# Recurrence of a hybrid decoder: both groups of four heads taken through the same stage in every visit

## Chip, core and metric

The kernel runs on one core of one Trainium2 chip. The metric is the device time of one execution in microseconds (us); lower is better. The engines that matter here are TensorE (PE for its matmuls, PEld for its weight loads), VectorE (DVE), ScalarE (ACT) and GpSimd (POOL).

## What is computed

The reference is a decoder trunk of two layers over 256 tokens and 1024 channels, batch 1. Each layer projects the normed input, runs a gated linear recurrence of 8 heads and a sliding-window attention of 16 heads beside each other, merges both under gates, and ends in a feed-forward block. The recurrence is the part that changes (C = 64 rows in a chunk, key and value width 128):

```python
b = jnp.cumsum(fi, axis=2)
o_inter = jnp.einsum('bhtk,bhkv->bhtv', qi * jnp.exp(b), state)
decay = jnp.exp(jnp.where(causal[:, :, None], diff, -jnp.inf))   # diff = b_t - b_s
scores = jnp.einsum('bhtk,bhsk,bhtsk->bhts', qi, ki, decay)
o_intra = jnp.einsum('bhts,bhsv->bhtv', scores, vi)
new_state = jnp.exp(b_last)[..., None] * state + jnp.einsum('bhsk,bhsv->bhkv', ki * jnp.exp(b_last - b), vi)
...
o_hg = rmsnorm(o_hg, hg_norm) * silu(hg);  y_a = o_hg @ w_pa
```

The kernel does not walk over chunks. It builds the whole matrix of decayed scores in levels: blocks of 4 rows, then 16, then pairs of 16, 32 and 64 rows, then the block of the second 128 tokens against the first 128; after each level q and k are multiplied by the decays that the next level needs.

## The kernel before

All large products are three passes of 128x128x512 matmuls over operands split in a high and a low part. The weights stream in from memory; ACT writes the high part of each piece (`wh`), DVE the low part (`wl`), four pieces ahead of the piece that TensorE reads (`used`, `take`, five buffers each). The functions of a layer are generators: `run` takes the main one (the projections) step by step, and a step is six wide matmuls in `form_a`. After every step it counts down the waits of the side generators (`start`), and runs a piece of each whose wait has ended. A number that a side generator yields is thus a distance in steps of the main work. Two side generators matter: `attention` and `recurrence`.

`attention` ends with `turn(3)`, a yield of `YB` = 3, `values(2)` and `values(3)` together, and a yield of 3. It keeps its scores in the tile `sp`. `recurrence` waits until the fourth `attend` was issued, issues `decays` for both groups of four heads (sigmoids, decays f, keys k), yields `YD` = 2, and polls until `attention` has ended. Each group has a generator `chain(g)`. Its pieces are, in order: pk (ACT copies q into the tile `pk`, DVE multiplies three products behind it), then for each stage one piece for TensorE and one for DVE, ACT and POOL. The stages are lb (blocks of 4 rows), lc (16 rows; its operand `p2` is made in the piece after lb, with a copy e1 by ACT and products e2, e3 by DVE), lv of 16, 32 and 64 rows, lx (the 128x128 block), o (output) and ot (transposition, then the split into `oT`).

Before the change group 0 runs one stage ahead of group 1. A visit issues the matmuls of both groups, group 1 first, then group 0's other work, waits a gap, then group 1's, and waits again (`GAPS`). So there are nine visits: lb0; lb1 with lc0; lc1 with lv16 of group 0; and so on to ot1 alone. Digits 0 and 1 behind a stage name its group below.

Within a visit (`pe_order` true) TensorE's instructions are pinned to the order of the program; DVE and ACT instructions are ordered at build time by a list scheduler, by readiness and then by program order, and every engine runs its list in that order on the chip. PSUM banks come by tag: group 0 uses two banks tagged `hg`, group 1 two tagged `at`, which the attention also uses. Group 0's `pk` and `p2` lie in the place of `sp`, group 1's in a place of their own (`pk`). Tiles tagged `hx` (the attention's `akv` and `kT`, later `sx` and `sq`) share four buffers.

Of the kernel before, what the change touches and what calls it, by code (L numbers as in the profile page):

```python
# [7 lines left out]
F32 = mybir.dt.float32  # L8
# [4 lines left out]
ALU = mybir.AluOpType  # L13
AX = mybir.AxisListType

P = 128
D = 1024
S = 256
# [9 lines left out]
EPS = 1e-6  # L28
MIN_F = 1e-30
NRAW, NW = 3, 5  # L30
YB, YD, YQ = 3, 2, 5
YN = (8,), (4, 3, 4), (4, 7), (4, 11)
GAPS = ((8,), (6, 7), (3, 5), (3, 3), (2, 3), (1, 2), (3, 2), (4, 2), (1,))
NEG = -1e30

C_HQ, C_HF, C_HI, C_HG, C_AQ, C_AK, C_GA, C_GB = 0, 1024, 2048, 3072, 4096, 5120, 5632, 6656
# [6 lines left out]
def trunk(ctx, tc, x, norm1, w_in, lb_logits, hg_norm, attn_sinks, w_pa, w_pb, w_o, norm2,  # L43
# [18 lines left out]
    V, A, G, T = (Ordered(e) for e in (nc.vector, nc.scalar, nc.gpsimd, nc.tensor))  # L62
# [9 lines left out]
    sm = ctx.enter_context(tc.tile_pool(name="sm", bufs=2))  # L72
# [3 lines left out]
    def psum(name, tag="mm"):  # L76
        return pp.tile([P, 512], F32, tag=tag, name=name, bufs=4 if tag == "mm" else 2)
# [4 lines left out]
    def ztile(shape, name, tag="z", dt=F32):  # L82
        return sm.tile(shape, dt, tag=tag, name=name, bufs={"z": 4, "hx": 4, "rp": 2}[tag])
# [345 lines left out]
    def layer(l, n1):  # L429
# [53 lines left out]
        def queries(g):  # L483
            for t in range(NT):
                ps = psum(f"qp{l}{t}{g}", "hg" if g else "at")
                for i in range(4):
                    T.transpose(ps[:, i * P:(i + 1) * P], aq[t][:, g * 512 + i * P:g * 512 + (i + 1) * P], ident)
                A.copy(qT[g][:, :, t * P:(t + 1) * P], ps.rearrange("p (i c) -> p i c", i=4))
# [74 lines left out]
        def attention():  # L563
            state["sp"] = sm.tile([P, 2, 4, 384], F32, tag="sp", name=f"sp{l}", bufs=1)
            for t in range(NT):
                rope(aq[t], QH, t)
            yield YQ
            queries(0)
            yield 2
            for n, gaps in enumerate(YN):  # L570
                visit = [values(n - 2, "mm")] if n > 1 else []
                together(*visit, attend(n))
                if n == 3:
                    state["last"] = True
                yield gaps[0]
                if n:
                    turn(n - 1)
                    yield gaps[1]
                if n == 1:
                    queries(1)  # L580
                    yield gaps[2]
            turn(3)
            yield YB
            together(values(2, "at"), values(3, "at"))
            yield 3

        def decays(g):
            f, q, k = fqk[g]
# [10 lines left out]
        def chain(g):  # L599
            f, q, k = fqk[g]  # L600
            tag, st = ("hg", "at")[g], st2[:, g]
            sd = sm.tile([P, 8, 32], F32, tag=f"sd{g}", name=f"sd{l}{g}", bufs=1)

            def mask(m, n, w):
                return cm[:, m:m + w].rearrange("p (o c) -> p o c", o=1).to_broadcast([P, n, w])

            pk = sm.tile([P, 32, 80], F32, tag=("sp", "pk")[g], name=f"pk{l}{g}", bufs=1)
            qb = q.rearrange("p h (b c) -> p (h b) c", c=32)
            f4 = f.rearrange("p h (b n o) -> p (h b) n o", n=8, o=4)
            q4 = q.rearrange("p h (b n o) -> p (h b) n o", n=8, o=4)  # L610
# [7 lines left out]
            for half in range(2):  # L618
                ps = psum(f"lb{l}{g}{half}", tag)[:, :320].rearrange("p (i c) -> p i c", c=80)
                for i in range(4):  # L620
                    h, t = 2 * half + i // 2, i % 2
                    for j in range(4):
                        ts_ = slice(t * P + 32 * j, t * P + 32 * j + 32)
                        T.matmul(ps[32 * j:32 * j + 32, i, :], k[:, h, ts_], pk[:, 8 * h + 4 * t + j, :],
                                 start=True, stop=True)
# [3 lines left out]
            for half in range(2):  # L629
                ps, sh = pss[half], sd[:, 4 * half:4 * half + 4, :]  # L630
# [14 lines left out]
            ku = k.rearrange("p h (n u m) -> p (h n) u m", u=2, m=2)  # L645
            V.tensor_tensor(ku[:, :, 0], ku[:, :, 0], fu[:, :, 1, 0:1].to_broadcast([P, 256, 2]), ALU.mult)
            V.tensor_tensor(fu[:, :, 0, 0], fu[:, :, 0, 0], fu[:, :, 1, 0], ALU.mult)
            p2 = sm.tile([P, 64, 24], F32, tag=("sp", "pk")[g], name=f"p2{l}{g}", bufs=1)
            qg = q.rearrange("p h (n b c) -> p (h n) b c", b=4, c=4)
            kg = k.rearrange("p h (n u b c) -> p (h n u) b c", u=2, b=2, c=4)  # L650
            fg = f.rearrange("p h (n b c) -> p (h n) b c", b=4, c=4)
# [5 lines left out]
            ps = psum(f"lc{l}{g}", tag)[:, :384].rearrange("p (i n c) -> p i n c", n=2, c=24)  # L657
            for i in range(8):
                h, t = i // 2, i % 2
# [18 lines left out]
            V.tensor_tensor(kg[:, :, 0], kg[:, :, 0], fu[:, :, 1, 0:1].to_broadcast([P, 64, 8]), ALU.mult)  # L678
            V.tensor_tensor(fu[:, :, 0, 0], fu[:, :, 0, 0], fu[:, :, 1, 0], ALU.mult)
            yield  # L680
            m = 16
            while m <= 64:
                nb = S // (2 * m)
                qv = q.rearrange("p h (n u m) -> p (h n) u m", u=2, m=m)
                kv_ = k.rearrange("p h (n u m) -> p (h n) u m", u=2, m=m)
                fv = f.rearrange("p h (n u m) -> p (h n) u m", u=2, m=m)
                ps = psum(f"lv{l}{g}{m}", tag)[:, :64 * 8 if m == 64 else 32 * 8].rearrange("p (i c) -> p i c", i=8)
                for i in range(8):
                    h, a = i // 2, i % 2 * P
                    if m == 16:  # L690
                        for j in range(4):
                            ts_ = slice(a + 32 * j, a + 32 * j + 32)
                            T.matmul(ps[32 * j:32 * j + 32, i, :], k[:, h, ts_], q[:, h, ts_], start=True, stop=True)
                    elif m == 32:
                        for j in range(2):
                            b = a + 64 * j
                            T.matmul(ps[64 * j:64 * j + 32, i, :], k[:, h, b:b + 32], q[:, h, b + 32:b + 64],
                                     start=True, stop=True)
                    else:
                        T.matmul(ps[0:64, i, :], k[:, h, a:a + 64], q[:, h, a + 64:a + P], start=True, stop=True)  # L700
                yield
                if m == 32:
                    for j in range(2):
                        A.copy(st[64 * j:64 * j + 32, :, 64 * j + 32:64 * j + 64], ps[64 * j:64 * j + 32])
                    for j in range(4):
                        pr = slice(32 * j, 32 * j + 32)
                        A.copy(st[pr, :, pr], sd[pr])
                elif m == 64:
                    A.copy(st[0:64, :, 64:128], ps[0:64])
                if m < 64:  # L710
                    bc = [P, 4 * nb, m]
                    V.tensor_tensor(qv[:, :, 1], qv[:, :, 1], fv[:, :, 0, 0:1].to_broadcast(bc), ALU.mult)
                    V.tensor_tensor(kv_[:, :, 0], kv_[:, :, 0], fv[:, :, 1, 0:1].to_broadcast(bc), ALU.mult)
                    V.tensor_tensor(fv[:, :, 0, 0], fv[:, :, 0, 0], fv[:, :, 1, 0], ALU.mult)
                else:
                    q4 = q.rearrange("p h (n m) -> p h n m", m=m)
                    k4 = k.rearrange("p h (n m) -> p h n m", m=m)
                    f4 = f.rearrange("p h (n m) -> p h n m", m=m)
                    V.tensor_tensor(q4[:, :, 3], q4[:, :, 3], f4[:, :, 2, 0:1].to_broadcast([P, 4, m]), ALU.mult)
                    V.tensor_tensor(k4[:, :, 0], k4[:, :, 0], f4[:, :, 1, 0:1].to_broadcast([P, 4, m]), ALU.mult)  # L720
                if m == 16:
                    V.copy_predicated(sd, mask(48, 8, 32), ps)
                yield
                m *= 2
            ps = psum(f"lx{l}{g}", tag).rearrange("p (i c) -> p i c", c=P)
            for h in range(4):
                T.matmul(ps[:, h, :], k[:, h, 0:P], q[:, h, P:S], start=True, stop=True)
            yield
            sx = ztile([P, 4, P], f"sx{l}{g}", "hx")
            A.copy(sx, ps)  # L730
            yield
            pss = []
            for t in range(NT):
                ps = psum(f"o{l}{g}{t}", tag).rearrange("p (h c) -> p h c", c=P)
# [9 lines left out]
            for t in range(NT):  # L744
                ps = pss[t]
# [23 lines left out]
        def recurrence():  # L769
            while "last" not in state:  # L770
                yield 1
            for g in range(2):
                decays(g)
            yield YD
            while atd[0] is not None:
                yield 1
            chains = [chain(g) for g in range(2)]
            next(chains[0])
            yield 2
            for n, gaps in enumerate(GAPS):  # L780
                live = [c for g, c in enumerate(chains) if 0 <= n - g < len(GAPS) - 1]
                pe_order[0] = True
                for c in live[::-1]:
                    next(c)
                pe_order[0] = False
                for c, gap in zip(live, gaps):
                    next(c, None)
                    if n == 0:
                        next(chains[1])
                    yield gap  # L790

        yield from proj("akv", lambda t, ps: evac_scaled(akv[t], ps, rs[t]), skew=l > 0, late=l == 0)
# [14 lines left out]
        for g in range(2):  # L807
            for dst in fqk[g][:2]:
                for b in range(2):
                    units = take(2)  # L810
                    for i in range(2):
                        ps = psum(f"pb{l}{g}{b}{i}")
# [201 lines left out]
        if end:  # L1014
            x1, ss, r = xs[1], nx.ss[:, 1], nx.r[1]
            tails = slice(512, 768), slice(768, D)
            for i, sl in enumerate(tails):
                ps = psum(f"last{i}")[:, :256]
# [117 lines left out]
```

## Time and profile before

| | us |
|---|---|
| median of 3 runs | 936.68 (935.9 to 936.97) |
| the profiled execution, device time | 936.02 |
| its span, first to last instruction | 934.3 |

The profiled execution spends 1.7 us outside its span. Durations below come from it. The layers show the same pattern twice, the second 459.4 us after the first; times are from the span's start. An operation's row holds the time from its start to the end of its write, which overlaps the next operation; what an engine really spends on it is the distance between starts. All matmul stretches run at a granted clock of 1.00 in the windows read below, so durations compare directly.

### The profile page before, as it was taken

How to read it: one execution, taken by the hardware profiler on the slowest of the kernel's cores; microseconds unless marked ns; L12 is line 12 of the kernel's file. 1: busy time of each engine (PE TensorE's matmuls, PEld its weight loads, DVE VectorE, ACT ScalarE, POOL GpSimd, SP SyncE). 2: the span in 40 equal slices, each digit the busy share in tenths (PEclk: the TensorE clock that was granted, in tenths of full speed). 3: DMA queues.
4: the chain of work that ended last, by engine and by line, in shares of the span. 5: the costliest groups of instructions: out<-in, count | busy, mean ns of one | idle time of the engine just before them, and what ended most of it. 6: DMA issues, size and time to landing. Idle time of an engine off the chain costs nothing.

```text
span 934.3 us, 14356 instructions
## 1 busy us (share of the span) xinstructions
PE 923.8 (99%) x5716; PEld 779.7 (83%) x5716; DVE 674.9 (72%) x1169; ACT 536.8 (57%) x906; POOL 21.1 (2%) x33
## 2 busy tenths in 40 slices
PE   8999999999999999999999999999999999999997
PEld 6878888888888888888888888888888888888885
DVE  5667679974778767766756677799667787667665
ACT  5665795465546555554555767945454565455553
POOL 2000000001000000000000000000010000000000
PEclk9999999999999999999999999999999999999999
DMA  7846435554545665566477444545545465556641
GB/s 277 236 150 212 136 98 167 191 178 135 172 144 184 195 202 186 181 190 203 164 157 238 135 136 140 176 151 179 169 155 183 158 201 183 181 184 204 195 139 46
DMA packets 111459, 161.40 MB, mean 173 GB/s; under 512 B 2976, under 2 KB 64736, under 8 KB 111392
## 3 DMA queue, kind: packets, MB, share of 16 engines
q1 hardware_dynamic: 110608, 159.38, 53.3%
q8 instruction: 45, 0.74, 0.3%
q10 hardware_dynamic: 560, 0.84, 0.3%
q0 software_dynamic: 224, 0.26, 0.1%
q14 instruction: 22, 0.18, 0.1%
HBM read 159.42 MB, written 1.05 MB: 172 GB/s over the span
## 4 chain that ended last, share of the span: by engine, by line
PE 89%; ACT 5%; DVE 4%; issue 0%; POOL 0%; DVEq 0%; ACTq 0%; POOLq 0%
PE pg L57 13%; PE pu L57 13%; PE acc L57 13%; PE pb L57 7%; PE gb L57 5%; PE ga L57 5%; PE v L57 5%; PE yb L57 5%; PE wo L57 5%; PE ya L57 5%; PE aq L57 5%; PE akv L57 2%; DVE wl L57 2%; ACT sp L57 1%; ACT wh L57 1%; PE o L57 1%
## 5 line engine op out<-in xcount | busy, mean ns | idle before, releaser
L57 DVE TENSOR_TENSOR wl<-raw,wh 128x1024 fp32r<-128x1024 f32 (+1 forms) x301 | 364.5, 1219 | 136.7 <-ACT wh L57 135.5
L57 ACT CAST wh<-raw 128x1024 fp32r<-128x1024 f32 (+1 forms) x301 | 314.0, 1049 | 171.8 <-PE acc L57 47.7
L57 PE MATMUL pu<-xx_n,wh 128*128 128x512 f32 x352 | 92.6, 393 | 0.0
L57 PE MATMUL pg<-xx_n,wh 128*128 128x512 f32 x352 | 92.1, 393 | 0.0
L57 PEld LDWEIGHTS pg<-xx_n,wh 128*128 128x128 f32 x352 | 63.2, 189 | 11.0
L57 PEld LDWEIGHTS pu<-xx_n,wh 128*128 128x128 f32 x352 | 63.1, 189 | 10.9
L57 PE MATMUL acc<-wh,ah 128*128 128x512 f32 x174 | 68.2, 392 | 0.0
L57 PE MATMUL acc<-wh,al 128*128 128x512 f32 x174 | 67.8, 391 | 0.0
L57 PE MATMUL acc<-wl,ah 128*128 128x512 f32 x174 | 67.8, 390 | 0.0
L57 PE MATMUL pb<-xx_n,wh 128*128 128x512 f32 x256 | 66.3, 396 | 0.0
L57 PEld LDWEIGHTS pb<-xx_n,wh 128*128 128x128 f32 x256 | 45.4, 189 | 8.9 <-DVE wl L57 0.7
L57 PEld LDWEIGHTS pg<-xx_n,wl 128*128 128x128 f32 x352 | 48.4, 190 | 4.1 <-ACT xx_n L57 0.6
L57 PEld LDWEIGHTS pu<-xx_n,wl 128*128 128x128 f32 x352 | 48.4, 190 | 3.6
L57 PE MATMUL pg<-xx_n,wl 128*128 128x256 f32 x352 | 50.3, 284 | 0.0
L57 PE MATMUL pu<-xx_n,wl 128*128 128x256 f32 x352 | 49.8, 283 | 0.0
L57 ACT COPY zg<-pg 128x256 f32<-128x256 f32 x44 | 16.4, 372 | 53.4 <-PE pg L57 53.4
L57 PE MATMUL ga<-wh,xx_n 128*128 128x512 f32 x128 | 41.5, 396 | 0.0
L57 PE MATMUL gb<-wh,xx_n 128*128 128x512 f32 x128 | 41.2, 393 | 0.0
L57 ACT ACTIVATE sp<-sp,stat 128x128 f32<-128x128 f32 (+1 forms) x64 | 28.2, 442 | 22.5 <-DVE stat L57 22.5
L57 PE MATMUL gate<-wh,xx_n 128*128 128x512 f32 x128 | 41.0, 394 | 0.0
L57 PE MATMUL v<-wh,xx_n 128*128 128x512 f32 x128 | 41.0, 394 | 0.0
L57 PE MATMUL aq<-wh,xx_n 128*128 128x512 f32 x128 | 40.3, 391 | 0.0
(240 smaller groups left out, 1662.9 us busy)
## 6 DMA issues: line engine op xcount, KB each, us to landing
raw<-in_w_in SPq DMA_DIRECT2D x58, 1024.0 KB, 5.3
raw<-in_w_gate SPq DMA_DIRECT2D x22, 1024.0 KB, 5.0
raw<-in_w_up SPq DMA_DIRECT2D x22, 1024.0 KB, 5.1
raw<-in_w_down SPq DMA_DIRECT2D x22, 1024.0 KB, 5.0
raw<-in_w_pb SPq DMA_DIRECT2D x8, 1024.0 KB, 5.0
raw<-in_w_pa SPq DMA_DIRECT2D x8, 1024.0 KB, 5.1
raw<-in_w_o SPq DMA_DIRECT2D x8, 1024.0 KB, 4.9
raw<-in_w_in SPq DMA_DIRECT2D x3, 512.0 KB, 6.2
```

The lines of the kernel that those rows point to most:

```text
L57: ins = call(*args, **kw)
```

## The change

Both groups go through the same stage in every visit, group 0 first. The level of 64 rows and the 128x128 block share a visit: the operands of the block, which were q and k after a multiplication that had to wait for the matmuls of the 64-row level, are now written into tiles of their own (`qx`, `kx`, tag `hx`) in the piece after the level of 32 rows, half by ACT copies and half by DVE products. Seven visits are left. The places of `pk` exchange: group 0 has the place of its own, group 1 that of `sp`. So group 0's pk piece is issued `YD` steps behind `decays`, before the attention has ended, and group 1's when it has. `attention` waits `YE` = 5 steps instead of 3 behind `turn(3)`, and no longer yields behind its last values. `GAPS` has a new list.

```diff
-YB, YD, YQ = 3, 2, 5
+YD, YE, YQ = 2, 5, 5
-GAPS = ((8,), (6, 7), (3, 5), (3, 3), (2, 3), (1, 2), (3, 2), (4, 2), (1,))
+GAPS = ((6, 6), (5, 5), (4, 4), (3, 3), (1, 2), (4, 4), (1, 1))
...
             turn(3)
-            yield YB
+            yield YE
             together(values(2, "at"), values(3, "at"))
-            yield 3
...
-            pk = sm.tile([P, 32, 80], F32, tag=("sp", "pk")[g], name=f"pk{l}{g}", bufs=1)
+            pk = sm.tile([P, 32, 80], F32, tag=("pk", "sp")[g], name=f"pk{l}{g}", bufs=1)
...
-            while m <= 64:
+            for m in (16, 32):
...
-                    V.tensor_tensor(q4[:, :, 3], q4[:, :, 3], f4[:, :, 2, 0:1].to_broadcast([P, 4, m]), ALU.mult)
-                    V.tensor_tensor(k4[:, :, 0], k4[:, :, 0], f4[:, :, 1, 0:1].to_broadcast([P, 4, m]), ALU.mult)
...
+                    qx, kx = (ztile([P, 4, P], f"{n}x{l}{g}", "hx") for n in "qk")
...
+                    A.copy(qx[:, :, 0:64], q4[:, :, 2])
+                    A.copy(kx[:, :, 64:P], k4[:, :, 1])
+                    V.tensor_tensor(qx[:, :, 64:P], q4[:, :, 3], f4[:, :, 2, 0:1].to_broadcast([P, 4, 64]), ALU.mult)
+                    V.tensor_tensor(kx[:, :, 0:64], k4[:, :, 0], f4[:, :, 1, 0:1].to_broadcast([P, 4, 64]), ALU.mult)
                 yield
...
+                T.matmul(ps[0:64, i, :], k[:, h, a:a + 64], q[:, h, a + 64:a + P], start=True, stop=True)
+            px = psum(f"lx{l}{g}", tag).rearrange("p (i c) -> p i c", c=P)
             for h in range(4):
-                T.matmul(ps[:, h, :], k[:, h, 0:P], q[:, h, P:S], start=True, stop=True)
+                T.matmul(px[:, h, :], kx[:, h, :], qx[:, h, :], start=True, stop=True)
             yield
             sx = ztile([P, 4, P], f"sx{l}{g}", "hx")
-            A.copy(sx, ps)
+            A.copy(st[0:64, :, 64:128], ps[0:64])
+            A.copy(sx, px)
...
             yield YD
+            chains = [chain(g) for g in range(2)]
+            next(chains[0])
+            yield 1
             while atd[0] is not None:
                 yield 1
-            chains = [chain(g) for g in range(2)]
-            next(chains[0])
-            yield 2
-            for n, gaps in enumerate(GAPS):
-                live = [c for g, c in enumerate(chains) if 0 <= n - g < len(GAPS) - 1]
+            next(chains[1])
+            yield 3
+            for gaps in GAPS:
                 pe_order[0] = True
-                for c in live[::-1]:
+                for c in chains:
                     next(c)
                 pe_order[0] = False
-                for c, gap in zip(live, gaps):
+                for c, gap in zip(chains, gaps):
                     next(c, None)
-                    if n == 0:
-                        next(chains[1])
                     yield gap
```

## Rows read from the trace of the kernel before

**Rows 1.** The page's first part, busy time, share of the span and instructions of each engine.
```profile
PE 923.8 (99%) x5716; PEld 779.7 (83%) x5716; DVE 674.9 (72%) x1169; ACT 536.8 (57%) x906; POOL 21.1 (2%) x33
```

**Rows 2.** TensorE's matmuls in order of time around the first visit of the first layer, and the same instruction of the second layer: start, duration, operation, tiles, shape, count, and in brackets the idle time before it and who ended it.
```profile
147.80 0.61 PE L57 MATMUL gate<-wh,xx_n 128*128 128x512 f32 x2
148.91 1.31 PE L57 MATMUL lb<-pk,k 128*32 128x80 f32 x64 [0.49 <-DVE pk L57]
150.15 0.50 PE L57 MATMUL gate<-wl,xx_n 128*128 128x512 f32 x1
150.49 0.62 PE L57 MATMUL gate<-wh,xx_n 128*128 128x512 f32 x2
...
608.29 1.31 PE L57 MATMUL lb<-pk,k 128*32 128x80 f32 x64 [0.50 <-DVE pk L57]
```

**Rows 3.** The same view at the last values of the attention and at later visits, with wide matmuls before and behind them.
```profile
138.29 2.87 PE L57 MATMUL pv<-sp,akv 128*64 128x256 f32 x32
141.09 0.50 PE L57 MATMUL gate<-wh,xx_n 128*128 128x512 f32 x1
...
160.71 0.39 PE L57 MATMUL gb<-wh,xx_n 128*128 128x512 f32 x1
161.03 1.31 PE L57 MATMUL lb<-pk,k 128*32 128x80 f32 x64
162.16 0.86 PE L57 MATMUL lc<-p,k 128*32 128x48 f32 x64
162.96 0.50 PE L57 MATMUL gb<-wh,xx_n 128*128 128x512 f32 x1
...
164.67 0.39 PE L57 MATMUL gb<-wl,xx_n 128*128 128x512 f32 x1
...
211.67 1.15 PE L57 MATMUL lv<-q,k 128*64 128x64 f32 x16
212.74 1.16 PE L57 MATMUL lx<-q,k 128*128 128x128 f32 x8
213.66 0.48 PE L57 MATMUL ga<-wh,xx_n 128*128 128x512 f32 x1
...
217.62 0.39 PE L57 MATMUL ga<-wh,xx_n 128*128 128x512 f32 x1
217.85 1.05 PE L57 MATMUL lx<-q,k 128*128 128x128 f32 x8
```

**Rows 4.** Busy time of each engine in three stretches (start:end, length, then each engine's busy time and instructions, granted clock, DMA share, GB/s): the end of the decays, from there to the operand of lc1, and the visits behind it.
```profile
128.70:139.02 10.32, 10.32 (x59) 8.41 (x58) 5.67 (x6) 10.32 (x16) 0.00 (x0) 1.00 0.30 100
139.02:178.95 39.93, 39.44 (x368) 32.53 (x364) 39.93 (x73) 22.11 (x26) 0.00 (x0) 1.00 0.53 175
180.86:211.67 30.81, 30.81 (x388) 25.28 (x387) 23.55 (x39) 16.71 (x25) 0.00 (x0) 1.00 0.54 173
```

**Rows 5.** DVE's instructions in order of time (columns as in rows 2): around pk, the first split of weights after the piece that follows lb0, the piece after lc0 (from 162.87 to 167.31, with one split of weights in it), and the last split of the second stretch of rows 4.
```profile
141.30 0.68 DVE L57 TENSOR_TENSOR att0l<-pv,att0h 128x512 fp32r<-128x512 f32 x1
141.90 1.40 DVE L57 SCALAR_TENSOR_TENSOR gate<-gate,r_n,gate 128x512 f32<-128x512 f32 x2
143.21 0.68 DVE L57 TENSOR_TENSOR att0l<-pv,att0h 128x512 fp32r<-128x512 f32 x1
...
144.94 0.95 DVE L57 TENSOR_TENSOR pk<-pk,f 128x768 f32<-128x768 f32 x1
145.87 1.23 DVE L57 TENSOR_TENSOR wl<-raw,wh 128x1024 fp32r<-128x1024 f32 x1
147.01 0.68 DVE L57 TENSOR_TENSOR pk<-pk,f 128x512 f32<-128x512 f32 x1
147.62 0.63 DVE L57 TENSOR_TENSOR q<-pk,f 128x256 f32<-128x256 f32 x1
148.15 0.61 DVE L57 TENSOR_TENSOR pk<-pk,f 128x256 f32<-128x256 f32 x1
...
156.68 1.22 DVE L57 TENSOR_TENSOR wl<-raw,wh 128x1024 fp32r<-128x1024 f32 x1
...
162.87 0.42 DVE L57 TENSOR_TENSOR q<-q,f 128x256 f32<-128x256 f32 x1
...
163.88 1.22 DVE L57 TENSOR_TENSOR wl<-raw,wh 128x1024 fp32r<-128x1024 f32 x1
...
167.31 1.22 DVE L57 TENSOR_TENSOR wl<-raw,wh 128x1024 fp32r<-128x1024 f32 x1
...
178.94 1.22 DVE L57 TENSOR_TENSOR wl<-raw,wh 128x1024 fp32r<-128x1024 f32 x1
```

**Rows 6.** DVE's costliest group of instructions in the second stretch of rows 4, out of the view that groups them: count, then busy time and mean ns of one, and the idle time before them.
```profile
L57 DVE TENSOR_TENSOR wl<-raw,wh 128x1024 fp32r<-128x1024 f32 x14 | 16.9, 1221 | 1.2 <-ACT wh L57 1.2
```

**Rows 7.** ACT's instructions in order of time (columns as in rows 2): the last keys, the transposed scores, the copies of q into pk, and copies of 256 elements per partition from SBUF and from PSUM.
```profile
134.51 1.16 ACT L57 ACTIVATE k<-f,ones 128x1024 f32<-128x1024 f32 x1
...
136.50 1.54 ACT L57 COPY sp<-pt 128x512 f32<-128x512 f32 x3
...
142.87 2.01 ACT L57 COPY pk<-q 128x1024 f32<-128x1024 f32 x2
...
189.40 0.41 ACT L57 COPY st<-sd 32x256 f32<-32x256 f32 x1
...
194.66 0.73 ACT L57 COPY st<-lv 32x256 f32<-32x256 f32 x2
```

More of the change, by code (lines that the diff above doesn't have):

```diff
@@ L647, in chain @@
             V.tensor_tensor(fu[:, :, 0, 0], fu[:, :, 0, 0], fu[:, :, 1, 0], ALU.mult)
-            p2 = sm.tile([P, 64, 24], F32, tag=("sp", "pk")[g], name=f"p2{l}{g}", bufs=1)
+            p2 = sm.tile([P, 64, 24], F32, tag=("pk", "sp")[g], name=f"p2{l}{g}", bufs=1)
             qg = q.rearrange("p h (n b c) -> p (h n) b c", b=4, c=4)
@@ L680, in chain @@
             yield
-            m = 16
-            while m <= 64:
+            for m in (16, 32):
                 nb = S // (2 * m)
@@ L686, in chain @@
                 fv = f.rearrange("p h (n u m) -> p (h n) u m", u=2, m=m)
-                ps = psum(f"lv{l}{g}{m}", tag)[:, :64 * 8 if m == 64 else 32 * 8].rearrange("p (i c) -> p i c", i=8)
+                ps = psum(f"lv{l}{g}{m}", tag)[:, :32 * 8].rearrange("p (i c) -> p i c", i=8)
                 for i in range(8):
@@ L693, in chain @@
                             T.matmul(ps[32 * j:32 * j + 32, i, :], k[:, h, ts_], q[:, h, ts_], start=True, stop=True)
-                    elif m == 32:
+                    else:
                         for j in range(2):
@@ L698, in chain @@
                                      start=True, stop=True)
-                    else:
-                        T.matmul(ps[0:64, i, :], k[:, h, a:a + 64], q[:, h, a + 64:a + P], start=True, stop=True)
                 yield
-                if m == 32:
+                bc = [P, 4 * nb, m]
+                V.tensor_tensor(qv[:, :, 1], qv[:, :, 1], fv[:, :, 0, 0:1].to_broadcast(bc), ALU.mult)
+                V.tensor_tensor(kv_[:, :, 0], kv_[:, :, 0], fv[:, :, 1, 0:1].to_broadcast(bc), ALU.mult)
+                V.tensor_tensor(fv[:, :, 0, 0], fv[:, :, 0, 0], fv[:, :, 1, 0], ALU.mult)
+                if m == 16:
+                    V.copy_predicated(sd, mask(48, 8, 32), ps)
+                else:
                     for j in range(2):
@@ L707, in chain @@
                         A.copy(st[pr, :, pr], sd[pr])
[L708 to L718, printed above, removed]
-                    V.tensor_tensor(q4[:, :, 3], q4[:, :, 3], f4[:, :, 2, 0:1].to_broadcast([P, 4, m]), ALU.mult)
-                    V.tensor_tensor(k4[:, :, 0], k4[:, :, 0], f4[:, :, 1, 0:1].to_broadcast([P, 4, m]), ALU.mult)
@@ L721, in chain @@
-                if m == 16:
-                    V.copy_predicated(sd, mask(48, 8, 32), ps)
-                yield
-                m *= 2
-            ps = psum(f"lx{l}{g}", tag).rearrange("p (i c) -> p i c", c=P)
+                    qx, kx = (ztile([P, 4, P], f"{n}x{l}{g}", "hx") for n in "qk")
+                    q4 = q.rearrange("p h (n m) -> p h n m", m=64)
+                    k4 = k.rearrange("p h (n m) -> p h n m", m=64)
+                    f4 = f.rearrange("p h (n m) -> p h n m", m=64)
@@ new lines, in chain @@
+                    A.copy(qx[:, :, 0:64], q4[:, :, 2])
+                    A.copy(kx[:, :, 64:P], k4[:, :, 1])
+                    V.tensor_tensor(qx[:, :, 64:P], q4[:, :, 3], f4[:, :, 2, 0:1].to_broadcast([P, 4, 64]), ALU.mult)
+                    V.tensor_tensor(kx[:, :, 0:64], k4[:, :, 0], f4[:, :, 1, 0:1].to_broadcast([P, 4, 64]), ALU.mult)
+                yield
+            ps = psum(f"lv{l}{g}64", tag).rearrange("p (i c) -> p i c", i=8)
+            for i in range(8):
+                h, a = i // 2, i % 2 * P
+                T.matmul(ps[0:64, i, :], k[:, h, a:a + 64], q[:, h, a + 64:a + P], start=True, stop=True)
```

## Prediction

> **What bounds the kernel now.** I read the page's busy times first: TensorE 99% of the span, DVE 72%, ACT 57% [rows 1]. That share alone says little, because a matmul's row overlaps the next one's, so I went to TensorE's matmuls in order of time. There the distance between starts is what counts: a wide matmul that follows another, or a 128x128 one that follows it, starts 0.23 us later (217.62 to 217.85) [rows 3], and six of them make a step of 1.36 us. Anything above 0.23 is lost. Around the recurrence there are two kinds of loss. Small ones stand at each change between full-width matmuls and those that fill 32 columns: 0.09 us going in (160.71 to 161.03) [rows 3] and 0.11 coming out (150.15 to 150.49) [rows 2]. One large one stands at the first visit: a gate matmul starts at 148.03 (the second of the pair from 147.80), the next instruction was due at 148.25, and lb0 starts at 148.91, late by 0.66, of which 0.09 is the change of form. So 0.57 us is a wait, and the row names DVE's pk as its end; the second layer repeats it [rows 2]. TensorE is thus the bound, and the change can only win what TensorE loses here. Then I read the engines by stretch: DVE is busy in all of the 39.93 us from 139.02 to 178.95, but only 5.67 of the 10.32 us before, and 23.55 of 30.81 us behind [rows 4]. In the first two thirds of the recurrence DVE is the second bound, right under TensorE.
>
> **The change, part by part.** The work is the same but for its order: as many matmuls, DVE products and ACT copies, save four ACT copies of 256 elements more per layer (two per group, for qx and kx).
>
> *The first visit's wait.* In both orders lb0 is issued eight steps behind turn(3) (3+3+2 before; 5+3 now), so its due time does not move. Before, group 0's copy into pk had to wait for the values to leave `sp`: copy at 142.87 [rows 7], products at 144.94, 147.01 and 148.15, done at 148.76, with a weight split (1.14) and a q product (0.53) between them [rows 5]. Now group 0's pk is free of the attention. Its copy can follow ACT's last keys, which end at 135.67 [rows 7], and its products (0.93+0.61+0.55, about 2.1 us) fit the 4.65 us in which DVE was idle up to 139.02 [rows 4]. lb0's wait goes: -0.57. What is late next is group 1's pk. The values move two steps (2.72 us) later, from 138.29 to 141.0, and leave `sp` 2.8 us later, at 143.8 [rows 3]. Then come one cast (0.59) and one copy (1.06) on ACT [rows 7], so about 145.5, then 2.1 us of products, with at most two splits between them: 147.6 to 149.9. lb1 is due at 148.34 plus lb0's 1.13 (161.03 to 162.16) [rows 3], 149.5. So 0 to 0.4 us of wait remain; I take 0.05, since group 1's products are traced ahead of the splits of the following steps.
>
> *Two visits fewer.* By count of visits, two times (0.09+0.11) = 0.4 us, plus the drain of their last small matmuls. But a block that is only 128x128 enters for nothing (217.62 to 217.85) [rows 3], so the visits with o and ot cost no entry. What costs is a change of form. Counted in the code they are 13 per layer before, 12 after: four visits of 32 columns with two each, none at o and ot, and now four in the shared visit (64 columns, 128, 64, 128) where the old order had three and two in the visits of lv32/lv64 and lv64/lx. The Trainium skill, TensorEngine Tiling (Array Packing), Key Properties, says that a change of tiling mode drains TensorE, while a change of tile does not; by that rule the two visits that go are worth one change, 0.1 us, and by counting visits 0.4. The rows side with the rule. I take -0.15 per layer, bounds -0.4 and 0.
>
> *The later operands.* ACT's copies for qx and kx: no row shows such a copy; the nearest take 0.41 (from SBUF, 256 elements) and 0.36 (from PSUM) [rows 7]. I take 0.4, so 1.6 us per layer, on an ACT that is busy for 16.71 of the 30.81 us in that stretch [rows 4]. Nothing of it is on the path: between lv32 and the shared visit lie six steps (8.2 us) and for group 1 three steps plus lv64 and lx of group 0, 1.99 us (211.67 to 213.66) [rows 3], 6.1 us, against 2.9 us of ACT copies and two splits of 1.05. If that cover is gone it costs at most those 2.9 us. From o to ot there are eight steps where five stood before; nothing is tight there.
>
> *The new squeeze.* From lb0 to lc1 there were 29-8 = 21 steps; now there are 12. Both pieces behind lb (call each B: the scores' masks, four q products, two levels of k and f, p2) must be done by DVE in that time, and TensorE's queue stops at lc until they are. lb now takes 2.26+0.3 us and starts at 148.34; 12 steps are 16.3 us; lc0 is due at 167.3, and lc1 0.7 later, at 168.0. DVE has 168.0-139.02 = 28.96 us from the time at which it saturated. Its work up to the old lc1 was 39.93 us [rows 4]: 13 splits at 1.13 (a fourteenth starts at its end [rows 6]) are 14.7; the last values 1.2; four gate products 2.6; two pk 4.1; the piece behind lc0 (162.87 to 167.31 less one split) 3.3, and an early q product 0.3 [rows 5]. The rest, 13.7, is 6.85 for each B. The new order needs by lc1: 1.2 + 2.6 + 13.7, group 1's pk 2.1, plus the splits. The splits that the program traces ahead of group 1's B are those up to the index that four pieces of lead allow at 14 steps behind turn(3): six from 139.02 on, 6.8 us. Sum 26.4. Group 0's pk may add up to 2.1, and each of three more splits that the scheduler slips in adds 1.13. So 26.4 to 31.9 against 28.96, and DVE also waits at times. Splits can give way: the one at 156.68 was read from 164.67 on, 6.8 us after it ended [rows 3, 5], the others more; a DVE that is late by a few splits stops nobody but lc. The wait at lc1 is 0 to 3 us; I take 0.2, since program order puts group 1's B ahead of the three late splits. From lc on it relaxes: 13.6 us of steps for 6.6 us of DVE work and five splits (5.7).
>
> **The sum.** Per layer -0.57 +0.05 -0.15 +0.2 = -0.47; two layers -0.9. Against the profiled execution's own 936.02 that is 935.1. The median of the runs is 0.66 above it, so on the median's scale 936.68 - 0.9 = **935.8 us**. Its own range: 934.7 (no wait left, 0.4 for the visits: -1.9) to 936.7 (lb and lc each some 0.4 late).
>
> **Rivals.** *lc is late (slower).* This is the squeeze with the splits queued ahead of group 1's B. TensorE runs its list in order, so a late lc holds every wide matmul behind it, as it did for 0.57 us at lb0 while gate matmuls were ready [rows 2]. If three more splits (3.4) and 1 us of idle DVE stand before p2, the need is 26.4+3.4+1+ half of group 0's pk (1.0) = 31.8, 2.9 us late: +5.7 in two layers, less 1.3 won: 941.0. It decides for slower from 1.6 us late per layer on. For it: DVE is at 100% in this stretch [rows 4], and before, splits did run between the products of pk [rows 5]. Against it: the splits' lead of 6.8 us and more. *lb is still late.* Group 1's pk takes over the wait, 0.4 to 0.5 us: 936.68 - 0.3 = 936.4. For it: ACT's cast and copy behind the values are a chain without slack. Against: lb0's 1.13 us ahead of lb1. *The early pk does not come early.* ACT is busy in all of the 10.32 us to 139.02 [rows 4]; if it takes group 0's copy behind the attention's, both pk stand in the way again, 2.1 us more DVE work before lb0, some 1.5 us late instead of 0.57: 936.68+2×(0.9-0.15) = 938.2. *The visits are worth more.* If each visit that goes saves its entry, exit and a drain, 0.6 per layer, and no new wait comes: 936.68 - 2×(0.57+0.6) = 934.3.
>
> **Chances.** Forecast 0.52, lc late 0.19, lb late 0.12, pk not early 0.06, visits worth more 0.11. About 0.2%, 1.9 us, is what a measurement of this kernel can tell from no change: faster is below 934.8, slower above 938.55. Faster: the last rival and the edge of the forecast, 0.15. Slower: most of lc late, part of the late pk, 0.21. Same 0.64. The range takes all but the low end of the last rival and the upper half of lc late: 934.5 to 939.6.
>
> **What would show it.** In the new trace lb0 should follow its gate matmul within 0.32 us, with no idle time that DVE ends, and DVE's first product of group 0's pk should start before 141. lc should be entered with 0.3 us as well; a bracket with DVE's p2, or ACT's e1 copy, there is the squeeze. Between lv64 and lx of the shared visit there should be changes of about 0.1 us. The prediction is wrong if lc waits over 1.6 us per layer, or if the time falls by more than TensorE's two losses named here.

## The result and the profile after

| | before | after |
|---|---|---|
| median, us | 936.68 (935.9 to 936.97) | 941.05 (940.79 to 942.0) |
| the profiled execution, us | 936.02 | 940.79 |
| its span, us | 934.3 | 939.0 |

The changed kernel takes 1.0049 of the time of before, 95% interval 1.0039 to 1.006. It is slower, by 0.49%, which is more than the 0.2% that the forecast took as the least that can be told from no change. The forecast was 935.8 us, with a range of 934.5 to 939.6, and both were wrong.

First, what answers to [rows 2] and [rows 3]: TensorE's matmuls in order of time at the first visit, at the second, and the same instructions of the second layer.

```profile
147.81 0.39 PE L57 MATMUL gate<-wh,xx_n 128*128 128x512 f32 x1
148.12 1.31 PE L57 MATMUL lb<-pk,k 128*32 128x80 f32 x64
150.68 1.31 PE L57 MATMUL lb<-pk,k 128*32 128x80 f32 x64 [1.24 <-DVE pk L57]
...
168.46 0.89 PE L57 MATMUL lc<-p,k 128*32 128x48 f32 x64
170.73 0.89 PE L57 MATMUL lc<-p,k 128*32 128x48 f32 x64 [1.38 <-DVE p L57]
...
612.49 1.31 PE L57 MATMUL lb<-pk,k 128*32 128x80 f32 x64 [1.24 <-DVE pk L57]
...
632.49 0.89 PE L57 MATMUL lc<-p,k 128*32 128x48 f32 x64 [1.32 <-DVE p L57]
```

Group 0's matmuls in lb follow the gate matmul after 0.31 us, with no bracket: the old wait is gone. Group 1's stand behind a wait in both visits (the bracket is the idle time of TensorE before the row), and the row names the engine and the tile each time. The waits do not replace one another; there are now two per layer where there was one.

DVE's queue says why. It answers to [rows 5]: first the products of group 1's pk, then from 163.80 on the end of group 1's piece that makes lc's operand p2.

```profile
145.60 1.29 DVE L57 TENSOR_TENSOR att0l<-pv,att0h 128x512 fp32r<-128x512 f32 x2
146.80 0.96 DVE L57 TENSOR_TENSOR pk<-pk,f 128x768 f32<-128x768 f32 x1
147.66 1.23 DVE L57 TENSOR_TENSOR wl<-raw,wh 128x1024 fp32r<-128x1024 f32 x1
148.80 0.69 DVE L57 TENSOR_TENSOR pk<-pk,f 128x512 f32<-128x512 f32 x1
149.40 0.61 DVE L57 TENSOR_TENSOR q<-pk,f 128x256 f32<-128x256 f32 x1
149.93 0.60 DVE L57 TENSOR_TENSOR pk<-pk,f 128x256 f32<-128x256 f32 x1
...
163.80 0.69 DVE L57 TENSOR_TENSOR k<-k,f 128x512 f32<-128x512 f32 x1
164.40 0.69 DVE L57 TENSOR_TENSOR f<-f 128x512 f32<-128x512 f32 x1
165.00 1.23 DVE L57 TENSOR_TENSOR wl<-raw,wh 128x1024 fp32r<-128x1024 f32 x1
166.14 0.69 DVE L57 TENSOR_TENSOR k<-k,f 128x512 f32<-128x512 f32 x1
166.74 0.64 DVE L57 TENSOR_TENSOR f<-f 128x256 f32<-128x256 f32 x1
167.28 1.23 DVE L57 TENSOR_TENSOR wl<-raw,wh 128x1024 fp32r<-128x1024 f32 x1
168.42 0.69 DVE L57 TENSOR_TENSOR p<-p,f 128x512 f32<-128x512 f32 x1
169.02 1.23 DVE L57 TENSOR_TENSOR wl<-raw,wh 128x1024 fp32r<-128x1024 f32 x1
170.16 0.43 DVE L57 TENSOR_TENSOR p<-p,f 128x256 f32<-128x256 f32 x1
```

Between products of group 1 that depend on each other stand others that the next visit does not need: for lb1 a weight split and a q product inside pk (1.67 us by distances of starts), for lc1 three weight splits (1.14 us each) inside the piece that makes p2. Two of the three windows below answer to [rows 4]. They show that DVE had no slack for these: it is busy in all of the 31.68 us up to lc1.

```profile
128.70:139.02 10.32, 10.32 (x53) 8.70 (x52) 6.82 (x9) 10.32 (x16) 0.00 (x0) 1.00 0.29 100
139.02:170.70 31.68, 29.09 (x324) 23.51 (x323) 31.68 (x57) 18.31 (x22) 0.00 (x0) 1.00 0.51 166
172.00:186.00 14.00, 14.00 (x124) 11.37 (x123) 12.90 (x24) 5.28 (x5) 0.00 (x0) 1.00 0.61 208
```

**Where the time went.** For each visit I took TensorE's time from 0.227 us behind the start of the last wide matmul before it to the point from which the wide matmuls stand 0.227 us apart again. I call it the cost of the visit; it includes waits and changes of form. Summed over the visits of the first layer it is 19.21 us before and 21.58 after (second layer 19.22 and 21.52). The difference of the two layers, 4.67, is the difference of the spans, 4.7, so the visits of the recurrence hold the whole loss. Where a visit is taken to end moves a sum by up to 0.1 us. Of after's sum, the visits lb and lc take 4.00 and 3.29.

### The profile page after: what moved, and what is told of

The parts are those of the page before. It is cut to its first block, busy times and chain, and to the rows that moved or that the text cites. A ratio compares the mean times of both kernels' runs of the same rounds, so it can differ in the third digit from the quotient of the medians.

```text
span 939.0 us, 14387 instructions
## 1 busy us (share of the span) xinstructions
PE 924.4 (98%) x5716; PEld 779.8 (83%) x5716; DVE 673.8 (72%) x1169; ACT 539.7 (57%) x914; POOL 19.7 (2%) x33
## 4 chain that ended last, share of the span: by engine, by line
PE 85%; DVE 9%; ACT 4%; issue 2%; POOL 0%; DVEq 0%; ACTq 0%; POOLq 0%
PE pg L57 13%; PE pu L57 13%; PE acc L57 13%; PE pb L57 7%; PE v L57 5%; PE wo L57 5%; PE ya L57 5%; PE ga L57 5%; PE aq L57 5%; PE yb L57 4%; DVE wl L57 3%; PE gb L57 2%; PE akv L57 2%; DVE q L57 1%; PE o L57 1%
```

## Experiments

Theory A: what TensorE waits for at lb1 and lc1 is one thing, DVE's queue up to group 1's p2, and the weight splits that stand between dependent products are what makes it late. Theory B: the two waits are separate, each with what stands right ahead of it, so that what is won at one is kept. Each run is compared with runs of the kernel before on the same chip (medians 936.11 to 936.2 us).

**places.** The kernel before, with the exchange alone: the places of pk change, group 0's pk is issued early, and the visits stay as they were.

```diff
-tag=("sp", "pk")[g], name=f"pk...      (p2 likewise)
+tag=("pk", "sp")[g], name=f"pk...
...
             yield YD
-            while atd[0] is not None:
-                yield 1
             chains = [chain(g) for g in range(2)]
             next(chains[0])
+            while atd[0] is not None:
+                yield 1
             yield 2
```

> The kernel before, with the exchange of the pk places alone (group 0's pk piece issued before the attention has ended; the staggered nine visits stay). Theory A (DVE's queue up to p2 is what TensorE waits for): lb0's wait of 0.57 us per layer goes and nothing takes its place, because in the old order p2 of group 1 was ready 1.9 us before its visit: 936.7 - 1.1 = 935.5 us. Theory B (the wait at a visit is the visit's own, each one additive): the same 935.5. If the early copy were not early at all: 936.7.

Measured: 935.07 us, ratio 0.9988 (0.9979 to 0.9998); in a second run beside later kernels:

> The kernel before with the two places of pk exchanged and group 0's pk issued early, once more, beside hold_step on the same chip: 935.1, and 0.2 to 0.4 us below hold_step.

935.04 us, 0.9988 (0.9979 to 0.9997), which is the same as hold_step below, not 0.2 to 0.4 less as expected. lb0 follows its gate matmul without a bracket, and the cost of the first visit falls from 2.00 to 1.45 us per layer:

```profile
148.26 0.39 PE L57 MATMUL gate<-wh,xx_n 128*128 128x512 f32 x1
148.58 1.31 PE L57 MATMUL lb<-pk,k 128*32 128x80 f32 x64
```

So the exchange brings what step one of the forecast said of it (0.55 against 0.57), and the loss comes from the rest of the change: the new visits and their gaps.

**hold_pk, hold_p2, hold_both.** The changed kernel, with work of DVE placed by hand. `issue_after` puts an instruction behind a given one in its engine's list. hold_pk does it for the weight splits, and the q products of the pieces behind, that are traced later than group 1's last pk product; hold_p2 for the splits traced later than the last product of group 1's p2; hold_both for all.

```diff
+    behind = [None]
+    def after(ins):
+        return tc.issue_after(ins) if ins is not None else nullcontext()
...
-                V.tensor_tensor(lo, raws[i], hi.bitcast(F32), ALU.subtract)
+                with after(behind[0]):
+                    V.tensor_tensor(lo, raws[i], hi.bitcast(F32), ALU.subtract)
...
             # hold_p2: behind the last product of p2 (hold_pk: behind the last of pk)
-            V.tensor_tensor(e3, e2[:, :, 1:2], ...)
+            last = V.tensor_tensor(e3, e2[:, :, 1:2], ...)
+            if g == 1:
+                behind[0] = last.ins
```

> The changed kernel, with the weight split and the q product that stand between the products of group 1's pk placed behind them on DVE. Both theories expect lb1's idle time of 1.24 us to go. Theory A: DVE has as much to do before p2 of group 1 as it had, and TensorE comes to lc earlier by what it won at lb, so lc1's idle time grows from 1.38 to about 2.8 us and the time stays at 941.0 (940.5 to 941.5). Theory B: lc1's idle time stays at 1.38, 941.0 - 2 x 1.43 = 938.2 us.

Measured: 942.98 us, 1.0075 (1.006 to 1.009). lb1 has no wait left (the visit costs 2.64 instead of 4.00), and lc1's grows from 1.38 to 2.55 us, in both layers. So theory B is out; theory A had the wait about right (2.8 expected) and the time wrong (941.0 expected). By the waits alone the kernel should take as long as the changed one, and it is 1.9 us slower. TensorE in order of time around lc, and the granted clock in windows behind it (columns as in [rows 4]), show the rest:

```profile
167.70 0.89 PE L57 MATMUL lc<-p,k 128*32 128x48 f32 x64
168.52 0.50 PE L57 MATMUL yb<-wh,att0h 128*128 128x512 f32 x1
171.57 1.16 PE L57 MATMUL lc<-p,k 128*32 128x48 f32 x64 [2.55 <-DVE p L57]
172.66 0.79 PE L57 MATMUL yb<-wl,att0h 128*128 128x512 f32 x1
173.25 0.63 PE L57 MATMUL yb<-wh,att0l 128*128 128x512 f32 x1
...
175.65 0.39 PE L57 MATMUL yb<-wh,att0l 128*128 128x512 f32 x1
```
```profile
172.00:173.00 1.00, 1.00 (x44) 0.88 (x33) 1.00 (x6) 0.00 (x0) 0.00 (x0) 0.51 0.50 51
173.00:174.00 1.00, 1.00 (x3) 0.81 (x3) 1.00 (x4) 0.00 (x0) 0.00 (x0) 0.50 0.96 356
174.00:176.00 2.00, 2.00 (x7) 1.52 (x7) 1.85 (x3) 0.75 (x1) 0.00 (x0) 0.64 0.86 329
176.00:178.00 2.00, 2.00 (x11) 1.65 (x10) 1.67 (x3) 0.30 (x1) 0.00 (x0) 1.00 0.00 0
```

Seven wide matmuls from 172.66 to 175.65 take 2.99 us instead of 7 × 0.227 = 1.59, and lc1's own 64 take 1.09 instead of 0.81: 1.68 us more, of which 0.11 is the usual way out of the 32-column form and the rest is lost at the lower clock. In the second layer nine wide matmuls take 3.65 us instead of 2.04, 1.61 us more. The execution of this trace took 944.51 us and is the slowest of four; the others, from 942.44 to 943.44, have no trace. Without both losses it would be at about 944.51 - 3.2 = 941.3, by this estimate, which is near theory A's 941.0. So of the 1.24 us of wait that are won at lb, 1.17 come back at lc.

> The changed kernel, with the three weight splits that stand between the products behind lb of group 1 placed behind p2 on DVE. p2 comes 3.4 us earlier less 0.7 for two q products that fill their places: ready at 167.8 where lc1 is due at 169.2. lc1's wait goes, lb1's stays, in both theories: 941.0 - 2 x 1.5 = 938.0 us. If the 1.38 us were ACT's e1 copy or a capacity that no order mends, 941.0.

Measured: 937.86 us, 1.0019 (1.0009 to 1.0028), as both theories expected; that ACT's copy e1, or a capacity that no order mends, made lc1 late is out (941.0 expected). The visit lc falls from 3.29 to 1.71 and is one row with no bracket; lb1's wait stays, at 1.26.

```profile
168.46 1.58 PE L57 MATMUL lc<-p,k 128*32 128x48 f32 x128
```

Here the last product of p2 starts at 167.70, before lc0, where p2 ended at 170.59 in the changed kernel.

> Both holds together. Theory A: lb1's wait goes, lc1 is due at 167.8 and p2 is ready at 167.8, so 0 to 0.3 us per layer are left: 935.2 to 935.9 us, below both kernels. Theory B: no wait left, 935.2 us. If the late splits (up to 4 us later) keep wide matmuls waiting, more than 937.

Measured: 936.43 us, 1.0004 (0.9994 to 1.0013). Both waits fall, but 0.54 us remain at lc1 in each layer. It is 0.5 above theory A's range, and not below the kernel before as theory A had it: with lb no longer late, TensorE is at lc1 earlier (168.1), and p2 is done at 168.5.

**lc_later and hold_step.** More time between lb and lc, without and with the hold.

```diff
 # lc_later, on the changed kernel
-GAPS = ((6, 6), (5, 5), (4, 4), (3, 3), (1, 2), (4, 4), (1, 1))
+GAPS = ((6, 8), (5, 5), (4, 4), (3, 3), (1, 2), (4, 4), (1, 1))
 # hold_step, on hold_both
+GAPS = ((6, 7), (5, 5), (4, 4), (3, 3), (1, 2), (4, 4), (1, 1))
```

> The changed kernel with two steps more between the visits lb and lc (gaps 6 and 8), nothing held back on DVE. Theory A1 (a time squeeze: 2.72 us more are enough for a p2 that is 1.3 us late): lc1's wait goes, lb1's 1.24 us stay, 941.05 - 2 x 1.6 = 937.9. Theory A2 (the list scheduler fills the two steps with the two splits that become ready in them, 2.3 us): the wait shrinks by 0.4 only, 940.2.

Measured: 937.68 us, 1.0015 (1.0006 to 1.0024). A1 holds: lc's visit costs 1.71, lb1's wait stays at 1.24, and DVE has the same three splits inside p2's piece (at 165.32, 167.60 and 169.34). So more time between the visits mends lc too, with no split moved: the time between them was too short for DVE's queue as it stood, and the list scheduler put no further split ahead of p2 into the two steps.

> hold_both with one step more between the visits lb and lc (gaps 6 and 7 in place of 6 and 6). Theory A (what is left in hold_both above the best order is DVE's p2, 0.54 us late per layer): one step gives DVE 1.36 us more and nothing new is traced ahead of it, so lc1 follows without idle time; 936.43 - 2 x 0.54 = 935.35, range 935.0 to 935.7. Theory B (DVE or ACT moves with the visit, so the wait stays): 936.4.

Measured: 935.04 us, 0.9987 (0.9978 to 0.9996), at the low end of what theory A said. In hold_step's order of matmuls both visits stand as one row, with no bracket; in DVE's order, the splits follow p2's last product:

```profile
148.15 2.49 PE L57 MATMUL lb<-pk,k 128*32 128x80 f32 x128
168.48 1.58 PE L57 MATMUL lc<-p,k 128*32 128x48 f32 x128
```
```profile
167.67 0.41 DVE L57 TENSOR_TENSOR q<-p,f 128x256 f32<-128x256 f32 x1
168.01 0.41 DVE L57 TENSOR_TENSOR p<-p,f 128x256 f32<-128x256 f32 x1
168.34 4.61 DVE L57 TENSOR_TENSOR wl<-raw,wh 128x1024 fp32r<-128x1024 f32 x4
```

The four splits run there one behind another for 4.6 us, and no matmul of the whole recurrence shows a bracket of over 0.1 us: the splits could give way. The kernel is now where places is, with the whole loss gone, so what the change wins then is the exchange of places alone, and the merged visits add nothing that these runs can tell.

**hold_split and hold_group.** What is a visit worth? hold_split takes hold_step's shared visit apart again; hold_group keeps it, and sorts it by form: the 64-row level of both groups, then the block of both.

```diff
 # both, in chain(g), between the matmuls of lv64 and of lx
+            yield
 # hold_split: A.copy of st and a second yield there, and one pair more in GAPS
-GAPS = (..., (3, 3), (1, 2), (4, 4), (1, 1))
+GAPS = (..., (3, 3), (1, 1), (1, 2), (4, 4), (1, 1))
 # hold_group: the fifth visit calls both groups twice
-            for gaps in GAPS:
+            for n, gaps in enumerate(GAPS):
...
-                for c in chains:
+                for c in chains * (2 if n == 4 else 1):
```

> hold_step with the level of 64 rows and the 128x128 block in visits of their own again, one step apart. Three prices of a visit. By changes of form, as in the prediction (0.1 us in, 0.1 us out, one more pair per layer): 935.35 + 2 x 0.15 = 935.65. By visits (0.6 us for each): 936.5. Nothing, as the sums of TensorE's time per visit in the traces of before and after say: 935.35.

> hold_split once more, beside hold_group on the same chip: 934.4, the shared visit's two halves at 2.21 and 1.79 us; by theory C the same as hold_group.

> hold_step with the shared visit sorted by form: the 64-row level of both groups, then the block product of both (two changes of form in the visit where four stood: 128 to 64 columns and back once). hold_step's shared visit took 4.34 us of TensorE, the two separate visits of hold_split 2.21 + 1.79 = 4.00. Theory C (a change of form is what costs, whoever's visit it is in): 4.00 us, 935.04 - 2 x 0.34 = 934.35. Theory D (each visit costs by itself, and sorting changes nothing): 4.34 us, 935.0. Theory E (both cost): under 3.9 us, 934.1.

Measured: hold_split 934.35 us, 0.9982 (0.9973 to 0.9991), and again 934.5, 0.998 (0.9971 to 0.9989); hold_group 934.24 us, 0.9979 (0.997 to 0.9988). None of the three prices that I wrote down for hold_split held: the kernel with one visit more is below hold_step. The shared visit in the changed kernel (hold_step has the same), then in hold_split, then in hold_group:

```profile
207.37 1.15 PE L57 MATMUL lv<-q,k 128*64 128x64 f32 x16
208.45 1.16 PE L57 MATMUL lx<-qx,kx 128*128 128x128 f32 x8
209.53 1.15 PE L57 MATMUL lv<-q,k 128*64 128x64 f32 x16
210.61 1.16 PE L57 MATMUL lx<-qx,kx 128*128 128x128 f32 x8
```
```profile
205.99 2.08 PE L57 MATMUL lv<-q,k 128*64 128x64 f32 x32
208.00 0.50 PE L57 MATMUL ga<-wh,xx_n 128*128 128x512 f32 x1
...
210.85 1.95 PE L57 MATMUL lx<-qx,kx 128*128 128x128 f32 x16
212.56 0.48 PE L57 MATMUL ga<-wh,xx_n 128*128 128x512 f32 x1
```
```profile
205.77 2.08 PE L57 MATMUL lv<-q,k 128*64 128x64 f32 x32
207.77 2.05 PE L57 MATMUL lx<-qx,kx 128*128 128x128 f32 x16
209.58 0.47 PE L57 MATMUL ga<-wh,xx_n 128*128 128x512 f32 x1
```

The costs are 4.34 us, 2.21 + 1.79 = 4.00, and 4.00. hold_split and hold_group have two changes of form there, the unsorted visit four. hold_split has one visit more than hold_group at the same cost, so this visit by itself costs nothing. Theory C holds, and the sum over a layer's visits falls from 18.62 to 18.31. The medians of hold_step and hold_group have intervals that overlap; the difference of 0.34 us per layer rests on the traces. hold_group has the lowest median of this study, 0.21% below before (0.12 to 0.30); it can't be told apart from hold_split.

## Why the prediction was wrong

**lb0's wait** went as forecast: group 0's pk starts on DVE at 136.64, and places gives the worth of the step alone. Two other terms of the sum failed, and a third was mis-sized.

**Group 1's pk** is the first step that failed: 0.05 us taken, 0 to 0.4 allowed, 1.24 measured. The copy on ACT came nearly as worked out (144.78 to 145.86, where the forecast had about 145.5). But the first product starts only at 146.80, because both att0l products (1.2 us) stood ahead of it, which the forecast left out here, and a split and a q product stand inside. The forecast allowed for two splits, but then took a value near zero "since group 1's products are traced ahead of the splits of the following steps". But the scheduler goes by readiness first and by the order of tracing second, and [rows 5] showed a split and a q product between pk's products already.

**The squeeze** is the second, and failed for the same reason, that program order would keep splits behind group 1's products: 0.2 taken, 0 to 3 allowed, 1.38 and 1.32 measured. The forecast put six splits ahead of p2 as the least; DVE's order in the changed kernel has ten between 139.02 and p2's end (11.3 us of work), of which the last three stand inside p2's own piece. Even hold_step, where nothing traced later may pass, has seven. The need came out at about 31.6 us (139.02 to p2's end at 170.59), near the forecast's upper end of 31.9: the range was right, and the value taken from it was wrong.

**lc late**, the rival at 941.0, was the mechanism, and it had a chance of 0.19: three more splits ahead of p2, DVE saturated, TensorE held in order. Its 2.9 us per layer agree with the measured 1.36 + 1.58 = 2.94 (the visit lb 4.00 against hold_step's and hold_pk's 2.64, the visit lc 3.29 against 1.71), though it had put them all at lc. That was half luck. A late lb delays TensorE on its way to lc and so hides part of the same lateness of DVE there. hold_pk shows it; with lb's wait removed it comes back at lc. The argument against the rival, that splits have lead enough to give way, was true and beside the point: hold_step shows that they can give way, and the changed kernel that nothing makes them.

**Two visits fewer** was mis-sized: -0.15 taken, 18.62 (hold_step) against 18.66 (places) measured, so -0.04, which is nothing within the 0.1 us above. A change of form is what costs: 0.34 us for two of them in the shared visit, 0.17 each, where the forecast took about 0.1. The Trainium skill, TensorEngine Tiling (Array Packing), Key Properties, says that a change of tiling mode drains TensorE and a change of tile does not. hold_split and hold_group agree with it in that a change of form costs. By the forecast's own count these two runs remove two more of its twelve.

With what was measured, the forecast's sum per layer is -0.55 (lb0's wait) + 1.36 (lb1) - 0.04 (visits) + 1.58 (lc1) = 2.35, or 4.7 in two layers, which is the difference of the spans.

**The later operands** cost nothing on the path, as forecast: ACT's copies for qx take 0.40 us and for kx 0.41, and in the shared visit lx follows lv after 1.08 us without a bracket.

**Whether the scheduler's readiness rule alone** put the splits there was not tested by itself and is argued; that their place costs the time is shown. What would have shown the failure ahead of time: the row of a split between two products of pk, taken as the rule and not as an accident.

## What to carry to other kernels

Where a stage is halved in length, count the second engine's whole queue up to the last operand, with every long operation that the order of before already shows inside a chain of dependent products. Program order is no promise when a scheduler goes by readiness. Work that is ready and has lead can be held behind the chain's last product by hand. When a wait is removed at one stage, look for it at the next stage that is fed by the same queue. Sort small matmuls within a visit by their form before merging visits.

## What was not expected of the hardware

In hold_pk TensorE did one wide matmul at 168.52, and then nothing until 171.57. Behind that the granted clock was 0.51 and 0.50 (the level of 1.2 GHz), the wide matmuls stood 0.43 us apart, and from 175.65 they stood at 0.23 again. In the second layer the stop was again 2.55 us; there lc1's matmuls still ran at full speed, and the clock was 0.61 from 636.00 to 637.00 and 0.50 from there to 639.00. In the changed kernel stops of 1.24 and 1.38 us left the clock at 1.00 (the windows above). So in this one execution a wait of 2.55 us cost about 1.6 us more than itself, in each layer. No run varied the length of the stop alone.
